# Weight sums of a seven-product feed-forward made by accumulating transfers, two pairs interleaved at its start

## The chip, the cores and the metric

The kernel runs on one core of one Trainium2 chip. The metric is device time in microseconds (us) of one execution; the time before is the median of three runs. The core has a matrix engine (TensorE, "PE" in the profile, with "PEld" for its weight loads), a vector engine (VectorE, "DVE"), an activation engine (ScalarE, "ACT"), a general engine (GpSimd, "POOL") and SyncE ("SP"), which here only issues transfers. Each engine takes its own instructions in program order and waits on semaphores for the others. PSUM is the memory that PE writes; it has eight banks.

## The reference

One inference step of a two-layer streaming encoder on 576 token columns (512 of a prompt, 64 of a sample), model width 1024. Each layer has a half-step feed-forward, a mixer (attention with a gated convolution in layer 0, a state-space mixer in layer 1), cross attention over 256 memory tokens, and a second half-step feed-forward:

```python
def swiglu(x, w_gu, w_down):
    gate, up = jnp.split(x @ w_gu, 2, axis=-1)
    return (jax.nn.silu(gate) * up) @ w_down

x = x + 0.5 * swiglu(rms_norm(x, ln_ffn1[l]), w_ffn1_gu[l], w_ffn1_down[l])
...
x = x + 0.5 * swiglu(rms_norm(x, ln_ffn2[l]), w_ffn2_gu[l], w_ffn2_down[l])
```

The hidden width is 2816, that is 22 tiles of 128. All arrays are float32.

## The kernel before

**Numbers as two parts.** PE is fed with pairs of numbers: `hi` (L136) lets ACT write a rounded copy, `lo` (L142) lets DVE write the rest. A product is then three matmuls per tile of 128 rows: high by high, high by low, low by high.

**Tokens in columns.** X is held transposed: eight tiles (f = 0 to 7) of 128 model rows by 576 columns. The columns are worked on in two halves of 288.

**Three of the four feed-forwards use seven products instead of eight.** For ffn2 of layer 0, ffn1 of layer 1 and ffn2 of layer 1 (`gain`, L496), a *pair* is a gate tile and an up tile of weights, 128 hidden columns each, `g1` and `g2`, each stored as 128 x 1024. Cutting the model rows into halves gives four weight blocks of 128 x 512: A11 and A12 in `g1`, A21 and A22 in `g2`. With two halves of the columns this is a 2 x 2 block product, and the kernel makes it in the Winograd form: seven products with four sums of weight blocks, four sums of x, and sums of the results. Product k uses weight `pr.src[k]`: k = 0 is A11, k = 2 is A12, k = 6 is A22, and k = 1, 3, 4, 5 are sums. `pair_ops` (L327) gives the matching halves of x: k = 0 and 1 use model tiles f < 4, k = 2 and 5 use f >= 4, and k = 3, 4, 6 use the sums `eh`, `el` of both. A product is 12 matmuls (`one`, L313) and writes one of the pair's three banks T, Y, W; `PLACE` lists them: k = 0, 3, 4, 6 go to T one after the other, 1 and 5 to Y, 2 to W. Before k = 3 may add to T, ACT must have copied what k = 0 left there, and so on; `pair_epi` (L534) makes these copies and additions after each product.

**Weight sums.** `pair_load` (L276) has SP load `g1` into a tile `r1` (tag wraw, three buffers that all other weights use too) and `g2` into `r2` (tag raw2, three buffers). `pair_sum` (L285) has DVE make the four sums, 128 x 512 each, into six buffers (tag ss). `run_steps` emits them up to six products ahead of `prep`, the place where ACT and DVE write the high and low parts of a product's weights. Two products share one weight buffer, of which there are three, so the parts are written some four products before PE uses them.

**Order.** `pair_steps` (L296) gives every product a place: pair n's product k stands at 7n + at[k], and all are sorted. A feed-forward is done in three parts of 6, 8 and 8 pairs (`PARTS`); each part is followed by eight down products of 48 (or 36) matmuls. In `run_steps` each product is a step: first the weights of later steps are loaded and prepared (`issue`, `ahead`, `prep`), then PE's matmuls are emitted, then the epilogue. At most three weight loads are open at a time (`st["open"]`).

**The start of a paired feed-forward.** It follows a layer whose last eight tiles of X come in the order 0, 4, 1, 5, 2, 6, 3, 7 (`PAIRED`). As each tile is done on PE, DVE adds it to X (L1315 after cross attention, L656 after a feed-forward), and `finalize_s` (L333) makes its high and low parts, the sums of x, and its squares. The first pair's k = 0 needs f = 0 to 3, its k = 2 needs f = 7 too. The norm's factor R is not known yet at that time: it is made beside the first products (`stats_tok`, ten matmuls of L471; `diag`, L444; `stats_bcast`, ten matmuls of L455), and the first pair's gate is multiplied by R later (`st["first"]`).

Of the kernel before, what the change touches and what calls it, by code (L numbers as in the profile page):

```python
# [9 lines left out]
F32 = mybir.dt.float32  # L10
# [3 lines left out]
ALU = mybir.AluOpType  # L14
# [7 lines left out]
HF = 288  # L22
# [48 lines left out]
class Pair:  # L71


    def __init__(self, g1, g2):
        self.g = (g1, g2)


class Kernel:
# [77 lines left out]
    def run_steps(self):  # L156
# [13 lines left out]
        def issue():  # L170
            i = st["issued"]
            g = items[i]
            if part[i]:
                if g.k == 0:
                    if self.fs is None or st["open"] >= 3 or i > st["prepped"] + 7:
                        return False
                    st["open"] += 1
                    self.pair_load(g.pair)
# [15 lines left out]
        def prep():  # L194
# [13 lines left out]
            if part[i]:  # L208
                c = slice(512 * place[i][1], 512 * place[i][1] + 512)
# [4 lines left out]
                self.lo(l, src, h)  # L214
            else:
# [7 lines left out]
        def ahead(n):  # L223
            while st["issued"] < min(st["prepped"] + n, N) and issue():
                pass
            while st["summed"] < min(st["issued"], st["prepped"] + 6):
                i = st["summed"]
                if part[i]:
                    self.pair_sum(items[i].pair, items[i].k)
                st["summed"] += 1  # L230

        used = 0
        for fn, gs, limit in self.steps:
# [6 lines left out]
            elif used < N:  # L240
                top = place[used][0] + (2 if gs else 1)
                while st["prepped"] < N and place[st["prepped"]][0] <= top:
# [3 lines left out]
                    ahead(8 if part[i] else 3)  # L246
                    prep()
                if here or (st["prepped"] < N and part[min(st["prepped"] + 2, N - 1)]):
                    ahead(8)
# [14 lines left out]
    def fs_open(self):  # L264
        if self.fs is None:
# [4 lines left out]
            fs["sum"] = self.phase_pool(fs, "fss", 6)  # L270
# [5 lines left out]
    def pair_load(self, pr):  # L276
        r1 = self.wraw.tile([128, WG], F32, tag="wraw", name="wraw")
        r2 = self.fs["raw"].tile([128, WG], F32, tag="raw2", name="raw2")
        self.nc.sync.dma_start(r1, pr.g[0])
        self.nc.sync.dma_start(r2, pr.g[1])  # L280
        a11, a12, a21, a22 = r1[:, :512], r1[:, 512:], r2[:, :512], r2[:, 512:]
        pr.src = [a11, None, a12, None, None, None, a22]
        pr.a21 = a21

    def pair_sum(self, pr, k):  # L285
        if k not in (1, 3, 4, 5) or pr.src[k] is not None:
            return
        for d in {3: (1,), 5: (3,)}.get(k, ()):
            self.pair_sum(pr, d)
        a11, s1, a12, s2, s3, s4, a22 = pr.src  # L290
        x, y, op = {1: (pr.a21, a22, ALU.add), 3: (s1, a11, ALU.subtract), 4: (a11, pr.a21, ALU.subtract),
                    5: (a12, s2, ALU.subtract)}[k]
        t = pr.src[k] = self.fs["sum"].tile([128, 512], F32, tag="ss", name="ss")
        self.nc.vector.tensor_tensor(t, x, y, op=op)  # L294

    def pair_steps(self, grans, ops, epi, late):  # L296
# [5 lines left out]
        for n, (g1, g2) in enumerate(grans):  # L302
# [30 lines left out]
    def finalize_s(self, f, gain):  # L333
# [14 lines left out]
        if f < 4:  # L348
            d = self.tmp("tb", HF)
            V.tensor_tensor(d, X[:, f, two], X[:, f, one], op=ALU.subtract)  # L350
# [6 lines left out]
        else:  # L357
# [5 lines left out]
            V.tensor_tensor(t[:, two], t[:, one], x0[:, one], op=ALU.add)  # L363
            self.hi(h, X[:, f], scale=g)
            V.scalar_tensor_tensor(u, X[:, f, one], g, t[:, two], op0=ALU.mult, op1=ALU.subtract)
            self.hi(e, t2)
            self.hi(self.eh[:, 2, k], u)
            self.lo(l, X[:, f], h, scale=g)
            self.lo(self.el[:, 0:2, k], t2, e)
            self.lo(self.el[:, 2, k], u, self.eh[:, 2, k])  # L370
# [158 lines left out]
    def ffn(self, gu, dn, gain_next, pairs=True, early=False):  # L529
# [4 lines left out]
        def pair_epi(k, pr, first, last, scaled):  # L534
# [5 lines left out]
            if k == 0:  # L540
# [4 lines left out]
                if "first" in st:  # L545
                    st["dg"] = self.diag(st["r"], "td")
            elif k == 1:
                self.hi(pr.tb[:, two], Y)
                if "first" in st:
                    st["R"] = self.stats_bcast(None, dg=st.pop("dg"), ps=self.banks[:, 6:8])  # L550
                    st.pop("first")()
            elif k == 3:
                self.hi(pr.tc[:, one], T)
                if first:
                    tt(pr.ta[:, two], Y, pr.tc[:, one], op=ALU.add)
# [1837 lines left out]
```

## Time and profile before

| | before |
|---|---|
| median of 3 runs | 2525.88 us (2524.17 to 2526.79) |
| the profiled execution | 2526.99 us, its span 2525.2 us |
| mean granted TensorE clock | 0.991 |
| DVE busy | 1741.2 us |
| POOL busy | 349.3 us |
| HBM read | 245.07 MB |

In a busy row of the page an engine's time is followed by its share of the span and its number of instructions. Matmuls overlap in the pipeline, so the duration of one in a timeline is longer than the time from one to the next. In the chain of waits a row is start, duration, engine, the tile written and the line; "x672" counts merged instructions. In a timeline the bracket at the end of a row gives how long the engine stood idle before it and what released it. In a table of windows each engine's busy time is followed by its number of instructions; the last three columns are granted clock, busy share of the DMA engines, and GB/s.

### The profile page before, as it was taken

The page shows a single profiled execution, that of the slowest core. Times are in us where ns is not written, and L with a number is a line of the kernel's source. Part 1 is how long each engine was busy: PE and PEld are TensorE (multiplying, and loading weights), DVE is VectorE, ACT ScalarE, POOL GpSimd, SP SyncE. Part 2 cuts the span into 40 slices and gives each one's busy share as a digit, 9 for nine tenths or more (in the row PEclk, how much of TensorE's full clock was granted, in tenths as well). Part 3 has the DMA queues.
Part 4 walks back from the last instruction along what each step waited for, and adds up shares of the span by engine and source line. Part 5 has one row for each costly group of instructions (what it writes and reads, how often), then busy time and mean ns, then how long its engine had stood idle before and what let it go on. Part 6 is the DMA issues. An engine that isn't in the chain of part 4 may idle for free.

```text
span 2525.2 us, 44952 instructions
## 1 busy us (share of the span) xinstructions
PE 2472.1 (98%) x18499; PEld 2435.2 (96%) x18499; DVE 1741.2 (69%) x2960; ACT 1074.6 (43%) x1847; POOL 349.3 (14%) x469
## 2 busy tenths in 40 slices
PE   8999999999999999999999999999999999999998
PEld 8998999999899999999999999999999999999998
DVE  5644658667875578786978785965743467787694
ACT  5322222334654455453545352542353355444353
POOL 1576235302420000000000000012310000000001
PEclk9999999999999999999999999999999999999999
DMA  4465653321134322322232323245872222232221
GB/s 149 93 187 184 155 123 122 121 93 36 37 113 136 120 84 70 115 79 97 76 101 61 108 83 101 85 143 167 289 244 84 84 93 84 76 110 84 100 84 64
DMA packets 112557, 279.95 MB, mean 111 GB/s; under 512 B 16304, under 2 KB 45152, under 8 KB 111712
## 3 DMA queue, kind: packets, MB, share of 16 engines
q1 hardware_dynamic: 112352, 277.08, 35.0%
q8 instruction: 145, 2.38, 0.4%
q14 instruction: 60, 0.49, 0.1%
HBM read 245.07 MB, written 31.97 MB: 110 GB/s over the span
## 4 chain that ended last, share of the span: by engine, by line
PE 75%; DVE 11%; DMA 5%; ACT 4%; POOL 2%; issue 2%; SPq 1%; ACTq 0%; POOLq 0%; DVEq 0%
PE banks L398 35%; PE banks L319 28%; PE banks L667 2%; PE banks L1912 2%; DVE wl L219 2%; DMA b<-in_ssm_bw 1%; PE banks L1293 1%; PE banks L1261 1%; PE banks L2188 1%; PE banks L1808 1%; ACT wh L138 1%; DVE ss L294 1%; POOL w L1414 1%; PE banks L1595 1%; DVE mx L999 1%
## 5 line engine op out<-in xcount | busy, mean ns | idle before, releaser
L138 ACT ACTIVATE wh<-wraw 128x1024 fp32r<-128x1024 f32 (+3 forms) x411 | 352.3, 861 | 331.9 <-PE banks L398 177.5
L219 DVE TENSOR_TENSOR wl<-wraw,wh 128x1024 fp32r<-128x1024 f32 (+2 forms) x264 | 321.6, 1221 | 171.9 <-ACT wh L138 169.7
L398 PE MATMUL banks<-hh,wh 128*128 128x288 f32 x1768 | 379.6, 296 | 2.6 <-ACT hh L138 1.8
L398 PE MATMUL banks<-hh,wl 128*128 128x288 f32 x1768 | 378.8, 296 | 2.8 <-DVE wl L219 2.8
L398 PE MATMUL banks<-hl,wh 128*128 128x288 f32 x1768 | 378.7, 296 | 0.5 <-DVE hl L144 0.5
L319 PE MATMUL banks<-xh,wh 128*128 128x288 f32 x1056 | 313.7, 297 | 7.9 <-ACT tb L138 4.0
L319 PE MATMUL banks<-xl,wh 128*128 128x288 f32 x1056 | 313.5, 297 | 3.6 <-DVE xl L146 3.4
L319 PE MATMUL banks<-xh,wl 128*128 128x288 f32 x1056 | 313.3, 297 | 0.4 <-DVE wl L144 0.4
L398 PEld LDWEIGHTS banks<-hh,wh 128*128 128x128 f32 x1768 | 284.7, 189 | 4.2 <-ACT hh L138 2.3
L398 PEld LDWEIGHTS banks<-hh,wl 128*128 128x128 f32 x1768 | 284.8, 189 | 3.2 <-DVE wl L219 3.2
L398 PEld LDWEIGHTS banks<-hl,wh 128*128 128x128 f32 x1768 | 284.8, 189 | 1.0 <-DVE hl L144 1.0
L398 PE MATMUL banks<-xh,wh 128*128 128x288 f32 x1232 | 269.3, 300 | 10.2 <-ACT wh L138 9.3
L398 PE MATMUL banks<-xh,wl 128*128 128x288 f32 x1232 | 267.4, 299 | 4.0 <-DVE wl L219 3.9
L398 PE MATMUL banks<-xl,wh 128*128 128x288 f32 x1232 | 266.1, 298 | 0.0
L319 PE MATMUL banks<-eh,wh 128*128 128x288 f32 x792 | 235.3, 297 | 1.0 <-DVE tc L579 1.0
L319 PE MATMUL banks<-el,wh 128*128 128x288 f32 x792 | 234.8, 296 | 0.0
L319 PE MATMUL banks<-eh,wl 128*128 128x288 f32 x792 | 234.5, 296 | 0.0
L144 DVE TENSOR_TENSOR wl<-ss,wh 128x512 fp32r<-128x512 f32 x264 | 181.4, 689 | 49.7 <-ACT wh L138 47.9
L398 PEld LDWEIGHTS banks<-xh,wh 128*128 128x128 f32 x1232 | 200.9, 191 | 12.2 <-ACT wh L138 9.6
L319 PEld LDWEIGHTS banks<-xh,wh 128*128 128x128 f32 x1056 | 200.0, 189 | 9.4 <-ACT tb L138 4.8
L398 PEld LDWEIGHTS banks<-xh,wl 128*128 128x128 f32 x1232 | 200.9, 191 | 5.7 <-DVE wl L219 5.5
L319 PEld LDWEIGHTS banks<-xl,wh 128*128 128x128 f32 x1056 | 199.9, 189 | 4.7 <-DVE xl L146 4.7
(539 smaller groups left out, 4927.0 us busy)
## 6 DMA issues: line engine op xcount, KB each, us to landing
wraw<-in_gu SPq DMA_DIRECT2D x110, 512.0 KB
raw<-in_gu SPq DMA_DIRECT2D x66, 512.0 KB
wraw<-in_dn SPq DMA_DIRECT2D x64, 512.0 KB
wraw<-in_dn SPq DMA_DIRECT2D x32, 384.0 KB
wraw<-in_win SPq DMA_DIRECT2D x17, 512.0 KB
wraw<-in_xq SPq DMA_DIRECT2D x16, 512.0 KB
wraw<-in_xk SPq DMA_DIRECT2D x16, 512.0 KB
wraw<-in_xv SPq DMA_DIRECT2D x16, 512.0 KB
```

Source lines behind the costliest of these rows:

```text
L138: self.nc.scalar.activation(out, in_, AF.Copy)
L144: self.nc.vector.tensor_tensor(out, in_, hi.bitcast(F32), op=ALU.subtract)
L219: self.lo_engine.tensor_tensor(l[:p, :n], t[:p, :n], h[:p, :n].bitcast(F32), op=ALU.subtract)
L294: self.nc.vector.tensor_tensor(t, x, y, op=op)
L319: mm(out, ww[:, ws], xx[:, kk], start=k < 3 and kk == 0 and pi == 0, stop=kk == 3 and pi == 2, skip_group_check=True)
L398: mm(ps[:M, h, :n], ww[:, k * M:(k + 1) * M], xx[:, k0 + k, h * n:(h + 1) * n], start=first and k == 0 and pi == 0, stop=last and k == kt ...
L667: nc.tensor.matmul(ps, ww[:, k * 128:(k + 1) * 128], xx[:, k, c0:c0 + n], start=k == 0 and pi == 0, stop=k == KT - 1 and pi == 2)
L999: V.reduce_max(mx[:m, qt:qt + 1], out, axis=AX.X)
L1261: mm(out, x[:, k, t * 128:t * 128 + m], y[:, k], start=k == 0 and pi == 0, stop=k == 1 and pi == 2)
L1293: mm(out, x[:, k, f * 128:(f + 1) * 128], y[:, k, ts], start=k == 0 and pi == 0, stop=k == 1 and pi == 2)
L1414: e.tensor_tensor(o_i, ar, bi, op=ALU.mult)
L1912: mm(ps[:, h, :HF], ww[:, k * 128:(k + 1) * 128], xx[:, k, h * HF:(h + 1) * HF], start=k == 0 and pi == 0, stop=k == 7 and pi == 2)
```

## The change

It concerns the three paired feed-forwards only.

- **Weight sums.** The signs of the Winograd form are turned, so that three of the four sums become plain additions. `pair_ahead` has POOL issue a transfer that adds A22, read from HBM, onto A21 in `r2` (for k = 1). After k = 1's parts are written, `pair_sums` has DVE make one sum (for k = 3, now two buffers), and POOL issue a transfer that adds A21, read from HBM, onto A11 in `r1` (for k = 4). After k = 2's parts, POOL issues one that adds the sum of k = 3, from SBUF, onto A12 in `r1` (for k = 5). Each is 128 x 512 float32, 256 KB. The signs are put right in `finalize_s` and in the down products' factor, -0.5.
- **Order.** The usual order of a pair becomes 0, 1, 2, 3, 5, 4, with its k = 6 between the next pair's 3 and 5. The first two pairs of a feed-forward are interleaved: first pair (a), second pair (b): a0 a1 b0 b1 a2 b2 a3 a5 b3 a4 b5 b4 a6 b6.
- **Look-ahead.** Loads may be issued when k = 0 stands up to 11 products ahead instead of 7; the sums' emission is five products ahead instead of six.
- **Norm factor.** Statistics still follow the first pair's k = 3; diag moves from the second pair's k = 0 to the first's k = 5, the broadcast and the first gate from the second's k = 1 to its k = 3.

```diff
-                    if self.fs is None or st["open"] >= 3 or i > st["prepped"] + 7:
+                    if self.fs is None or st["open"] >= 3 or i > st["prepped"] + 11:
...
                 self.hi(h, src)
                 self.lo(l, src, h)
+                self.pair_sums(g.pair, g.k)
...
-            while st["summed"] < min(st["issued"], st["prepped"] + 6):
+            while st["summed"] < min(st["issued"], st["prepped"] + 5):
                 i = st["summed"]
                 if part[i]:
-                    self.pair_sum(items[i].pair, items[i].k)
+                    self.pair_ahead(items[i].pair, items[i].k)
...
-                    ahead(8 if part[i] else 3)
+                    ahead(12 if part[i] else 3)
...
-            fs["sum"] = self.phase_pool(fs, "fss", 6)
+            fs["sum"] = self.phase_pool(fs, "fss", 2)
...
+        pr.src = [pr.r1[:, one], pr.r2[:, one], pr.r1[:, two], None, pr.r1[:, one], pr.r1[:, two], pr.r2[:, two]]
+
+    def pair_ahead(self, pr, k):
+
+        if k == 1:
+            self.nc.gpsimd.dma_start(pr.r2[:, pr.half[0]], pr.g[1][:, pr.half[1]], accum_op=ALU.add)
+
+    def pair_sums(self, pr, k):
+
+        one, two = pr.half
+        if k == 1:
+            t = pr.src[3] = self.fs["sum"].tile([128, 512], F32, tag="ss", name="ss")[:, one]
+            self.nc.vector.tensor_tensor(t, pr.r2[:, one], pr.r1[:, one], op=ALU.add)
+            self.nc.gpsimd.dma_start(pr.r1[:, one], pr.g[1][:, one], accum_op=ALU.add)
+        elif k == 2:
+            self.nc.gpsimd.dma_start(pr.r1[:, two], pr.src[3], accum_op=ALU.add)
...
-            at = {0: 0, 1: 1, 3: 3, 2: 4, 5: 5, 4: 6, 6: 9}
-            if n == len(grans) - 1:
-                at = {0: 0, 1: 1, 3: 3, 2: 4, 4: 5, 5: 6, 6: 7}
-            elif late and n == 0:
-                at = {0: 0, 1: 1, 2: 2, 5: 3, 3: 4, 4: 7.5, 6: 10.5}
+            at = {0: 0, 1: 1, 2: 2, 3: 3, 5: 5, 4: 6, 6: 11}
+            if late and n < 2:
+                at = ({0: 0, 1: 1, 2: 4, 3: 6, 5: 7, 4: 9, 6: 12}, {0: -5, 1: -4, 2: -2, 3: 1, 5: 3, 4: 4, 6: 6})[n]
+            elif n == len(grans) - 1:
+                at = {0: 0, 1: 1, 2: 2, 3: 3, 5: 5, 4: 6, 6: 9}
...
-            V.tensor_tensor(d, X[:, f, two], X[:, f, one], op=ALU.subtract)
+            V.tensor_tensor(d, X[:, f, one], X[:, f, two], op=ALU.subtract)
...
-            V.tensor_tensor(t[:, two], t[:, one], x0[:, one], op=ALU.add)
+            V.scalar_tensor_tensor(t[:, two], t[:, one], -1.0, x0[:, one], op0=ALU.mult, op1=ALU.subtract)
...
+            elif k == 3:
+                self.hi(pr.tc[:, one], T)
+                if first:
+                    st["r"] = self.stats_tok(self.acc, self.ones, 1.0, ps=self.banks[:, 6:8])
+                elif "first" in st:
+                    st["R"] = self.stats_bcast(None, dg=st.pop("dg"), ps=self.banks[:, 6:8])
+                    st.pop("first")()
...
+                tt(pr.ta[:, two], Y, pr.tc[:, one], op=ALU.add)
                 if first:
                     st["first"] = lambda: (gate(), self.defer(silu, 1))
-                    return
-                tt(pr.ta[:, two], Y, pr.tc[:, one], op=ALU.add)
-                if last:
+                    st["dg"] = self.diag(st["r"], "td")
+                elif last:
```

More of the change, by code (lines that the diff above doesn't have):

```diff
@@ L75, in __init__ @@
         self.g = (g1, g2)
+        self.kw = g1.shape[1] // 2
+        self.half = slice(0, self.kw), slice(self.kw, 2 * self.kw)
 class Kernel:
@@ L208, in prep @@
             if part[i]:
-                c = slice(512 * place[i][1], 512 * place[i][1] + 512)
+                c = slice(512 * place[i][1], 512 * place[i][1] + g.pair.kw)
                 src = g.pair.src[g.k]
@@ L245, in run_steps @@
                         break
-                    ahead(8 if part[i] else 3)
+                    ahead(12 if part[i] else 3)
                     prep()
                 if here or (st["prepped"] < N and part[min(st["prepped"] + 2, N - 1)]):
-                    ahead(8)
+                    ahead(12)
             ws = [handles.pop(used + k) for k in range(len(gs))]
@@ L276, in pair_load @@
     def pair_load(self, pr):
[L277 to L286, printed above, removed]
-            return
[L288 to L294, printed above, removed]
+        n = 2 * pr.kw
+        pr.r1 = self.wraw.tile([128, WG], F32, tag="wraw", name="wraw")
+        pr.r2 = self.fs["raw"].tile([128, WG], F32, tag="raw2", name="raw2")
+        self.nc.sync.dma_start(pr.r1[:, :n], pr.g[0])
+        self.nc.sync.dma_start(pr.r2[:, :n], pr.g[1])
+        one, two = pr.half
[4 more added lines that the diff above has]
+    def pair_sums(self, pr, k):
+        one, two = pr.half
+        if k == 1:
[4 more added lines that the diff above has]
+            self.nc.gpsimd.dma_start(pr.r1[:, two], pr.src[3], accum_op=ALU.add)
     def pair_steps(self, grans, ops, epi, late):
@@ L362, in finalize_s @@
             V.scalar_tensor_tensor(t[:, one], X[:, f, two], g, x0[:, two], op0=ALU.mult, op1=ALU.subtract)
-            V.tensor_tensor(t[:, two], t[:, one], x0[:, one], op=ALU.add)
+            V.scalar_tensor_tensor(t[:, two], t[:, one], -1.0, x0[:, one], op0=ALU.mult, op1=ALU.subtract)
             self.hi(h, X[:, f], scale=g)
-            V.scalar_tensor_tensor(u, X[:, f, one], g, t[:, two], op0=ALU.mult, op1=ALU.subtract)
+            V.scalar_tensor_tensor(u, X[:, f, one], g, t[:, two], op0=ALU.mult, op1=ALU.add)
             self.hi(e, t2)
-            self.hi(self.eh[:, 2, k], u)
+            self.hi(self.eh[:, 2, k], u, scale=-1.0)
             self.lo(l, X[:, f], h, scale=g)
             self.lo(self.el[:, 0:2, k], t2, e)
-            self.lo(self.el[:, 2, k], u, self.eh[:, 2, k])
+            self.lo(self.el[:, 2, k], u, self.eh[:, 2, k], scale=-1.0)
         if f == 0:
@@ L544, in pair_epi @@
                 self.hi(pr.tb[:, one], T)
-                if "first" in st:
-                    st["dg"] = self.diag(st["r"], "td")
             elif k == 1:
                 self.hi(pr.tb[:, two], Y)
[L549 to L554, printed above, removed]
-                    tt(pr.ta[:, two], Y, pr.tc[:, one], op=ALU.add)
-                    st["r"] = self.stats_tok(self.acc, self.ones, 1.0, ps=self.banks[:, 6:8])
             elif k == 2:
@@ L655, in down @@
                 if last and pairs:
-                    V.scalar_tensor_tensor(self.h2(x), ps[:, :, :HF], 0.5, self.h2(x), op0=ALU.mult, op1=ALU.add)
+                    V.scalar_tensor_tensor(self.h2(x), ps[:, :, :HF], -0.5, self.h2(x), op0=ALU.mult, op1=ALU.add)
                 else:
                     t = self.tmp("tc")
-                    V.scalar_tensor_tensor(self.h2(t), ps[:, :, :HF], 0.5, self.h2(st["R"]), op0=ALU.mult, op1=ALU.mult)
+                    V.scalar_tensor_tensor(self.h2(t), ps[:, :, :HF], -0.5 if pairs else 0.5, self.h2(st["R"]), op0=ALU.mult, op1=ALU.mult)
                     V.tensor_tensor(x, x, t, op=ALU.add)
@@ L671, in down_out @@
                 x = self.X[:, f, c0:c0 + n]
-                V.scalar_tensor_tensor(x, ps, 0.5, x, op0=ALU.mult, op1=ALU.add)
+                V.scalar_tensor_tensor(x, ps, -0.5, x, op0=ALU.mult, op1=ALU.add)
                 if f == 0 and c0 == 0:
```

2 lines of the change are left out of this document (removed).

## The prediction

> **What bounds the kernel now.** I read the page's engine shares first, then the chain that ended last in order of time, then the timelines of DVE, ACT and PE around the starts of the three paired feed-forwards.
>
> ```profile
> PE 2472.1 (98%) x18499; PEld 2435.2 (96%) x18499; DVE 1741.2 (69%) x2960; ACT 1074.6 (43%) x1847; POOL 349.3 (14%) x469
> ```
>
> PE leaves 53 us of the span idle, so nothing here can gain more than a few per cent. The chain says where it can. A piece that is PE for tens of microseconds has no gap in it:
>
> ```profile
> 935.73 0.99 PE banks L471 x10
> 936.72 4.97 PE banks L319 x36
> 941.68 1.25 PE banks L455 x10
> ...
> 954.60 43.15 PE banks L319 x324
> 997.75 38.40 PE banks L398 x288
> 1036.14 89.02 PE banks L319 x672
> 1125.16 51.19 PE banks L398 x384
> ...
> 1393.14 38.40 PE banks L398 x288
> ...
> 2191.75 38.40 PE banks L398 x288
> ```
>
> 672 matmuls in 89.02 us are 56 products of 12, so a product takes 1.59 us and a pair of seven 11.13. From 954.60 to the end of that feed-forward PE never waits, so fewer DVE sums can gain nothing there. What is left is its first part, six pairs, 42 products: 42 x 1.5896 = 66.76 us, plus the ten small matmuls of L471 (0.99) and of L455 (1.25) that each feed-forward has once: 69.0 us without a wait. The first product starts here (PE timeline):
>
> ```profile
> 919.84 0.19 PEld L319 LDWEIGHTS banks<-xh,wh 128*128 128x128 f32 x1
> 1316.26 0.19 PEld L319 LDWEIGHTS banks<-xh,wh 128*128 128x128 f32 x1
> 2113.37 0.19 PEld L319 LDWEIGHTS banks<-xh,wh 128*128 128x128 f32 x1
> ```
>
> The part ends where the down products begin: 997.75 - 919.84 = 77.9, 1393.14 - 1316.26 = 76.9, 2191.75 - 2113.37 = 78.4 us. Against 69.0 that is 8.9, 7.9 and 9.4: **26.2 us lost at three starts**, all that this change can win from PE. Two kinds of loss, seen in the first:
>
> ```profile
> 926.84 0.19 PEld L319 LDWEIGHTS banks<-xh,wh 128*128 128x128 f32 x1 [1.72 <-ACT xh L140]
> 928.37 0.29 PEld L319 LDWEIGHTS banks<-xl,wh 128*128 128x128 f32 x1 [1.33 <-DVE xl L146]
> 930.34 0.29 PEld L319 LDWEIGHTS banks<-xh,wh 128*128 128x128 f32 x1 [1.47 <-ACT tb L138]
> ```
> ```profile
> 929.00:939.00 10.00, 8.88 (x53) 8.63 (x53) 8.26 (x21) 5.79 (x13) 0.00 (x0) 0.72 0.01 2
> ```
>
> PE waits for the last tile of x (f = 7) and for the copy of T, and the granted clock falls to 0.72 for the ten microseconds after. Behind that stands a late DVE:
>
> ```profile
> 893.29 1.23 DVE L219 TENSOR_TENSOR wl<-wraw,wh 128x1024 fp32r<-128x1024 f32 x1 [0.20 <-ACT wh L138]
> 899.45 0.69 DVE L294 TENSOR_TENSOR ss<-raw 128x512 f32<-128x512 f32 x1 [4.93 <-DMA raw<-in_gu]
> ...
> 901.51 0.75 DVE L1315 TENSOR_TENSOR X<-banks,X 128x576 f32<-128x576 f32 x1
> ...
> 907.35 0.76 DVE L1315 TENSOR_TENSOR X<-banks,X 128x576 f32<-128x576 f32 x1
> ...
> 912.54 0.75 DVE L1315 TENSOR_TENSOR X<-banks,X 128x576 f32<-128x576 f32 x1
> ...
> 917.25 0.69 DVE L144 TENSOR_TENSOR wl<-wraw,wh 128x512 fp32r<-128x512 f32 x1
> ...
> 919.66 0.75 DVE L1315 TENSOR_TENSOR X<-banks,X 128x576 f32<-128x576 f32 x1
> ...
> 923.43 0.68 DVE L144 TENSOR_TENSOR wl<-wraw,wh 128x512 fp32r<-128x512 f32 x1
> 924.03 0.69 DVE L294 TENSOR_TENSOR ss<-ss,wraw 128x512 f32<-128x512 f32 x1
> 925.23 0.75 DVE L1315 TENSOR_TENSOR X<-banks,X 128x576 f32<-128x576 f32 x1
> ...
> 929.94 0.69 DVE L144 TENSOR_TENSOR wl<-ss,wh 128x512 fp32r<-128x512 f32 x1
> ```
>
> The out products take 48 matmuls, 6.4 us (51.19 / 8), a tile. Counted back from 919.84, PE is done with f = 5, 2, 6, 3, 7 at 894.2, 900.6, 907.0, 913.4, 919.8; DVE adds them to X at 901.51, 907.35, 912.54, 919.66, 925.23, some 5.4 to 7.3 late. It stood 4.93 us in front of a pair sum that waited for its weights, and made six sums, the first at 899.45, the last at 924.03.
>
> **The change, part by part.** *Sums off DVE.* Three feed-forwards have 22 pairs each. 3 x 66 sums of 0.69 (the row at 899.45) = 137 us leave DVE. In the gapless stretches they hide under PE and are worth nothing. At a start they count: the sum that stood 4.93 us now comes behind its own pair's second product, and 2 sums instead of 6 stand before f = 7. New DVE timetable from the distances of the rows above (such instructions follow each other every 0.60, 923.43 to 924.03): f = 5 from 894.2, 5.84 of work (901.51 to 907.35): 900.0. f = 2 from 900.6, 5.19: 905.8. f = 6 from 907.0, 4.71: 911.7, then the first pair's two low parts and its one sum, 1.8: 913.5. f = 3, 3.77 (919.66 to 923.43): 917.3, the second pair's three: 919.1. f = 7 is then added as PE delivers it, 919.8 instead of 925.23.
>
> *Products in another order.* Before, two products (k = 0, 1) need only the tiles f < 4; the third needs f = 7. Now the two pairs give four: 4 x 1.59 = 6.4 us of work from 919.8 to 926.2. xh and xl of f = 7 come 1.6 and 3.1 us behind its add (926.84 and 928.37 against 925.23), at 921.4 and 922.9. So neither stops PE. k = 3 adds onto T; five products lie between it and the first pair's k = 0 where three did, so the copy of T is done too. Without an idle PE I take the clock to stay at the 1.00 it has elsewhere.
>
> *What is moved.* The broadcast of R (L455) comes two products after the statistics (3.18 us), where 4.97 lay between. diag is late by:
>
> ```profile
> 939.24 1.03 DVE L444 TENSOR_SCALAR dg<-ident,tko 128x128 f32<-128x128 f32 x5
> ```
>
> It ends 3.55 us after L471 does (936.72), so some 0.4 us of waiting. gate and silu of the first pair move with it; its k = 6 ends four products after the broadcast, 6.4 us for a multiplication and an activation. The next user of the first pair's banks now comes one product (1.59 us) after its k = 6, not three and a half; it waits for one DVE product, and with the sums gone DVE has no queue there. The sign changes put one instruction of DVE for another of its size. Loads may be issued eleven products ahead instead of seven, but three buffers limit them as before. The last pair of each part has k = 6 behind k = 4 instead of k = 5, which gives its silu one product more. Together I leave **1.5 us a start** on PE.
>
> *Three accumulating transfers a pair, 256 KB each, issued by POOL.* POOL does nothing in these stretches, so its queue is free; a pair's two late transfers stand there ahead of the next pair's early one, which waits only for a load that landed long before. No row shows such a transfer. Call L the time from the last reader's end to its landing. Bounds:
>
> ```profile
> L1584 POOL TENSOR_TENSOR ca<-x,sr 128x1152 f32<-128x1152 f32 x8 | 21.6, 2704 | 68.3 <-DMA s5wout<-ca 55.5 <-DVE wl L219 12.8
> ```
> ```profile
> b<-in_ssm_bw SPq DMA_DIRECT2D x8, 512.0 KB
> ...
> s5y<-yw SPq DMA_DIRECT2D x3, 592.0 KB
> ...
> yr<-s5y SPq DMA_DIRECT2D x24, 74.0 KB
> ```
> ```profile
> 178.31 3.50 DMA b<-in_ssm_bw
> ...
> 1827.74 2.24 DMA yr<-s5y
> ...
> 1837.65 9.66 DMA s5y<-yw
> ```
>
> Low: nothing for POOL and a 74 KB transfer, 2.24 us. High: its longest instruction 2.7 + the slow 592 KB store 9.66 = 12.4 us. An accumulate reads its 256 KB and the target's 256 KB, so the 512 KB load at 3.50 is nearest; with 1.0 for POOL I take **L = 4.5 us**. The Trainium skill, DMA: Bandwidth & Descriptors, section on the anatomy of one DMA, fits about 2.0 us plus size over 436 GB/s for a transfer issued by GpSimd, an estimate of 2.6 us; no run here shows it, and by it the sum stays as it is.
>
> Who waits for L? The transfer into the second half of the first weight row (for k = 5) is sent behind k = 2 and used three products later; that is the short one. k = 4's has five, and k = 1's is sent ahead. hi of k = 5 waits at the head of ACT, and the copies out of the banks and the next hi stand behind it. In steady state the weights run ahead:
>
> ```profile
> 1069.55 0.41 ACT L138 ACTIVATE tb<-banks 128x288 f32<-128x288 f32 x1 [0.15 <-PE banks L319]
> ```
> ```profile
> 1069.71 0.69 DVE L144 TENSOR_TENSOR wl<-wraw,wh 128x512 fp32r<-128x512 f32 x1
> ```
>
> k = 0 ended just before the copy at 1069.55; k = 2 then started about 4.77 later, 1074.3, and its low part was ready at 1070.4: 3.9 ahead.
> ```profile
> L138 ACT ACTIVATE wh<-ss x264: 613/622/638, 916.4 to 2450.2; 128x512 fp32r<-128x512 f32 x132
> ```
>
> So L may be 3.9 + 3 x 1.59 - 1.3 (hi and lo of k = 5, 0.62 and 0.69) = 7.4 us before PE waits, once a pair. At a start the low part of k = 2 follows the 4.71 of f = 7 (925.23 to 929.94): done at 919.8 + 4.7 + 0.7 = 925.2; PE wants k = 5 at 919.8 + 7 x 1.59 + 0.99 = 931.9, so L may be 5.4. At 4.5 both hold and the transfers cost nothing; their cover is that lead.
>
> **Sum.** 26.2 - 0.4 (a load starts 0.14 before its matmul) - 3 x 1.5 = 21 us won. The profiled execution took 2526.99 (span 2525.2 and 1.8 around it), 1.1 above the median of the runs, 2525.88; from the median: **2505 us**.
>
> **Rivals.** *The wait comes back in part*: L between 5.4 and 7.4. Each start loses up to 2.0 us at the first pair's k = 5, as much at the second's, and the clock may fall again, about 4 x 3 = 12 us: **2517**. For it: the start has the least lead, and two pairs' megabytes are loading then. Against: the loads are issued long before.
>
> *The transfers become the bound, slower*: L above 7.4 us at k = 5. It decides from 7.4 + 21/66 = 7.7 us on; at L = 9 each of 66 pairs loses 1.6, 106 us, against a gain that shrinks to some 10: **2620**; at the high bound, 66 x 5.0, above 2840. For it: one high row, 9.66, a third queue of requests on DMA engines that also carry 1 MB of weights a pair. Against: those are busy a quarter of the time here, with POOL at zero:
>
> ```profile
> 1060.00:1110.00 50.00, 50.00 (x379) 50.00 (x379) 44.71 (x81) 29.08 (x56) 0.00 (x0) 1.00 0.27 85
> ```
>
> *POOL is held off while DVE computes*: DVE is busy 44.71 of 50, after the change 44.7 x (1 - 3 x 0.6 / 9.95) = 36.6, in runs of up to 8 us. A transfer that had to wait out such a run adds about 4 us: L = 8.5, 66 x 1.1 = 73, **2585**. No row speaks for or against it, since POOL does nothing in these stretches; its one high price would be that of the case before. The Trainium skill, SBUF — State Buffer, on who interferes with whom, has GpSimd's descriptor writing blocked by DVE's two-port modes but, by inference, not by tensor_tensor; nearly all of DVE's work here is that, so by the page this rival falls away. No run here shows it.
>
> *DVE was not the cause*: the starts stay late because PE delivers f = 7 last and four products do not cover what follows: **2525**, no change. Against: the timetable above.
>
> **Chances.** Forecast, gain over 15 us: 0.52. Part of it: 0.20. No change: 0.08. Transfers the bound: 0.13. POOL held off: 0.07. About 0.2% (5 us) is what a measurement of this kernel tells from no change. Faster 0.71, same 0.09, slower 0.20. The range holds the first three: from 26.2 us won with nothing left, **2499**, to 5 above the median, **2531**; the slower cases lie outside.
>
> **What would show it.** Right: no idle PE between the first product of a feed-forward and its down products, 69 to 71 us instead of 77 to 78; clock 1.00 there; X for f = 7 added within 1 us of PE's end; DVE near 1605 us busy; waits of ACT for the accumulates short. Wrong: ACT's hi of k = 5 or DVE behind it waiting for the transfer in every pair, with PE gaps at 11-us intervals; POOL's issues spread over microseconds; PE waiting for L444 or for the bank copies at the starts.

## The result and the profile after

The changed kernel takes **2562.44 us**, median of 4 runs (2562.05 to 2565.37), beside 2526.09 (2524.17 to 2526.79) for the kernel before: ratio 1.0148, 95% interval 1.0130 to 1.0165. It is 36 us slower; 2505 with a range of 2499 to 2531 was predicted. The profiled execution took 2562.18, span 2560.1, mean granted clock 0.989.

Page of the kernel after: engine shares and the issues of POOL's transfers, whose last number is the median from issue to landing.

```profile
PE 2477.1 (97%) x18499; PEld 2438.1 (95%) x18499; DVE 1628.7 (64%) x2762; ACT 1066.3 (42%) x1847; POOL 524.1 (20%) x667
...
raw<-in_gu POOLq DMA_DIRECT2D x66, 256.0 KB, 5.5
wraw<-in_gu POOLq DMA_DIRECT2D x66, 256.0 KB, 4.1
wraw<-ss POOLq DMA_DIRECT2D x66, 256.0 KB, 4.5
```

DVE has lost 112 us of work and the transfers land about as estimated, yet the span grew. PE has the same 18499 instructions, so it stands still somewhere new. Waits of PE in the kernel after (total, times, longest), then one of ACT:

```profile
PE banks L327 <- DVE tc L584: 35.5, 12, 4.3
...
PE banks L327 <- ACT tb L141: 2.5, 4, 1.0
...
ACT wh L141 <- DMA wraw<-ss: 140.3, 61, 6.4
```

The first row is the loss. L584 is DVE's addition of what k = 4 left in bank T to the copy that ACT made before. Nine of its twelve waits are 3.4 to 4.3 us long, 34.1 together, one at the end of each of the nine parts (three feed-forwards of three parts); the other three are 0.5 us each, at the starts. ACT waits 140 us for the transfer of k = 5, and in the middle of a part of eight pairs PE takes no harm from it. Windows of the kernel after: PE busy, PEld, DVE, ACT, POOL, granted clock, DMA share, GB/s.

```profile
1060.00:1110.00 50.00, 50.00 (x379) 50.00 (x378) 36.86 (x67) 28.24 (x55) 10.56 (x12) 1.00 0.71 157
```

PE is gapless there as before, DVE went from 44.71 to 36.86 (36.6 was predicted), the share of the DMA engines from 0.27 to 0.71.

The end of a part in the kernel after, here the second part of the first paired feed-forward: PE, then DVE, then ACT.

```profile
1124.61 0.29 PE L327 MATMUL banks<-eh,wl 128*128 128x288 f32 x1
1128.29 0.41 PE L327 MATMUL banks<-eh,wh 128*128 128x288 f32 x1 [3.39 <-DVE tc L584]
```
```profile
1123.91 0.46 DVE L568 TENSOR_TENSOR ta<-ta,R 128x288 f32<-128x288 f32 x1
1126.64 1.23 DVE L223 TENSOR_TENSOR wl<-wraw,wh 128x1024 fp32r<-128x1024 f32 x1 [2.27 <-ACT wh L141]
1127.78 0.45 DVE L584 TENSOR_TENSOR tc<-banks,tb 128x288 f32<-128x288 f32 x1
```
```profile
1124.40 0.68 ACT L571 ACTIVATE ta<-ta 128x576 f32<-128x576 f32 x1 [2.89 <-DVE ta L568]
1124.99 0.67 ACT L141 ACTIVATE hh<-td 128x576 fp32r<-128x576 f32 x1
1125.57 1.04 ACT L141 ACTIVATE wh<-wraw 128x1024 fp32r<-128x1024 f32 x1
```

The last matmul of k = 4 starts at 1124.61. k = 6 goes to the same bank T, directly behind it, and has to wait until L584 has read the bank. L584 itself is free to run at 1124.9, but DVE works in program order, and in front of it stands the low part of a down product's weights (L223), which waits 2.27 us for its high part on ACT. ACT in turn made the silu that follows k = 5 first (L571, released by DVE at 1124.4), then the high part of a hidden tile (hh), then the weights' 1.04 us. So the bank is read at 1127.78 instead of some three microseconds earlier. In the kernel before, k = 5, which goes to bank Y, stood between the two, and the same read came in time (kernel before, PE's last matmul of k = 4 and first of k = 6, then DVE):

```profile
1121.66 0.30 PE L319 MATMUL banks<-eh,wl 128*128 128x288 f32 x1
...
1123.39 0.32 PE L319 MATMUL banks<-eh,wh 128*128 128x288 f32 x1
```
```profile
1120.79 1.23 DVE L219 TENSOR_TENSOR wl<-wraw,wh 128x1024 fp32r<-128x1024 f32 x1 [2.13 <-ACT wh L138]
...
1122.80 0.45 DVE L579 TENSOR_TENSOR tc<-banks,tb 128x288 f32<-128x288 f32 x1
```

The wide low part waits 2.13 us there too, but that wait is over before k = 4 is done: no silu stands in front of its high part on ACT, because the silu belongs to k = 5 and comes later (L566 at 1125.94). The read ends at 1123.25, 1.29 us behind k = 4 and 0.14 before k = 6 starts. So the swap did two things: it took away the 1.59 us of k = 5 that covered the read, and it made the read later, 3.3 to 4.3 us behind k = 4 at the nine ends of the kernel after, 0.8 to 1.3 in the kernel before.

PE's time from the first product of a part to the last, from the starts in its timeline (the floor is 69.0 for a first part with its 20 small matmuls, 89.0 for one of eight pairs):

| | first parts | parts of eight pairs |
|---|---|---|
| before | 77.6, 76.6, 78.1 | 89.0, six times |
| after | 77.3, 78.7, 77.1 | 92.7, 94.7, 94.0, 94.7, 94.0, 94.7 |

The six long parts lose 30.8 us, the first parts 0.8: they win at the start nearly what they lose at the end. The spans of the two profiled executions, 2525.2 and 2560.1, differ by 34.9 us. Of the 3.3 that are left, nearly 3 lie in the down products behind the parts, the rest in other stages.

### The profile page after: what moved, and what is told of

Its sections match the earlier page's. It is cut to its first block, busy times and chain, and to the rows that moved or that the text cites. A ratio compares the mean times of both kernels' runs of the same rounds, so it can differ in the third digit from the quotient of the medians.

```text
span 2560.1 us, 45526 instructions
## 1 busy us (share of the span) xinstructions
PE 2477.1 (97%) x18499; PEld 2438.1 (95%) x18499; DVE 1628.7 (64%) x2762; ACT 1066.3 (42%) x1847; POOL 524.1 (20%) x667
## 5 line engine op out<-in xcount | busy, mean ns | idle before, releaser
L141 ACT ACTIVATE wh<-wraw 128x512 fp32r<-128x512 f32 (+2 forms) x543 | 430.3, 803 | 506.5 <-PE banks L406 229.7
L223 DVE TENSOR_TENSOR wl<-wraw,wh 128x1024 fp32r<-128x1024 f32 (+2 forms) x264 | 322.4, 1224 | 168.6 <-ACT wh L141 166.4
L327 PE MATMUL banks<-xh,wh 128*128 128x288 f32 x1056 | 312.0, 295 | 1.3 <-ACT tb L141 0.8
L327 PE MATMUL banks<-xh,wl 128*128 128x288 f32 x1056 | 311.4, 295 | 0.0
L327 PE MATMUL banks<-xl,wh 128*128 128x288 f32 x1056 | 310.9, 294 | 0.0
L327 PE MATMUL banks<-eh,wh 128*128 128x288 f32 x792 | 238.8, 302 | 37.2 <-DVE tc L584 35.5
L147 DVE TENSOR_TENSOR wl<-wraw,wh 128x512 fp32r<-128x512 f32 x264 | 181.4, 688 | 144.9 <-ACT wh L141 131.7
L327 PE MATMUL banks<-el,wh 128*128 128x288 f32 x792 | 237.6, 300 | 0.0
L327 PE MATMUL banks<-eh,wl 128*128 128x288 f32 x792 | 237.3, 300 | 0.0
L327 PEld LDWEIGHTS banks<-xh,wh 128*128 128x128 f32 x1056 | 198.4, 188 | 2.6 <-DVE td L605 1.4
```

Of the source, the lines that this page charges most:

```text
L141: self.nc.scalar.activation(out, in_, AF.Copy)
L147: self.nc.vector.tensor_tensor(out, in_, hi.bitcast(F32), op=ALU.subtract)
L223: self.lo_engine.tensor_tensor(l[:p, :n], t[:p, :n], h[:p, :n].bitcast(F32), op=ALU.subtract)
L327: mm(out, ww[:, ws], xx[:, kk], start=k < 3 and kk == 0 and pi == 0, stop=kk == 3 and pi == 2, skip_group_check=True)
```

## The experiments

Theory A: the loss is the order at the end of each part (k = 4 and k = 6 back to back in bank T). Theory B, the rival: the accumulating transfers are the bound, that is the waits of ACT for them and the third stream of requests.

| label | start | sums | end of part | median us | ratio to before, 95% |
|---|---|---|---|---|---|
| after | interleaved | transfers | 5, 4, 6 | 2562.4 | 1.0148 [1.0130, 1.0165] |
| e1_k4_first | interleaved | transfers | 4, 5, 6 | 2524.6 | 0.9995 [0.9985, 1.0005] |
| e2_before_k5_first | as before | DVE | 5, 4, 6 | 2570.6 | 1.0189 [1.0174, 1.0205] |
| e3_dve_sums | interleaved | DVE | 4, 5, 6 | 2539.7 | 1.0063 [1.0050, 1.0075] |
| e4_usual_start | usual | transfers | 4, 5, 6 | 2508.0 | 0.9935 [0.9922, 0.9947] |
| e8_dve_usual | usual | DVE | 4, 5, 6 | 2524.6 | 0.9995 [0.9986, 1.0005] |
| e12_usual_start_alone | usual | transfers | 5, 4, 6 | 2550.9 | 1.0099 [1.0076, 1.0122] |
| e7_k6_earlier | usual | transfers | 4, 5, 6, pair before sooner | 2521.8 | 0.9989 [0.9979, 1.0000] |
| e11_rest_sooner | usual | transfers | 4, 5, 6, a low part sooner | 2501.6 | 0.9901 [0.9886, 0.9915] |
| e9_pool_one | usual | transfers, 1 copy ahead | 4, 5, 6 | 2509.5 | 0.9939 [0.9922, 0.9955] |
| e10_pool_three | usual | transfers, 3 copies ahead | 4, 5, 6 | 2634.6 | 1.0419 [1.0404, 1.0434] |

### The order at the end of a part

**e1_k4_first**, the kernel after with the last pair's k = 4 put ahead of its k = 5, nothing else:

```diff
             elif n == len(grans) - 1:
-                at = {0: 0, 1: 1, 2: 2, 3: 3, 5: 5, 4: 6, 6: 9}
+                at = {0: 0, 1: 1, 2: 2, 3: 3, 4: 5, 5: 6, 6: 9}
```

> The changed kernel, but in the last pair of each of the nine parts k = 4 stands before k = 5, as it did before the change. Theory A (the order at the end of a part): the changed kernel's PE waits 35.5 us in all before k = 6 for the addition of L584 that reads T, 3.5 to 4.5 us at each of the nine part ends, and some 8 to 11 us more go to the low clock after it; with a product between k = 4 and k = 6 both go, 2562 - 46 = 2516, and every part of eight pairs takes 89.0 us again. Theory B (the accumulating transfers are the bound: ACT waits 140 us for them): nothing of that goes, 2555 to 2565.

Measured: 2524.59 us (2519.53 to 2528.97, 11 runs), 37.9 below the kernel after (46 were expected), and not to be told from the kernel before. The parts of eight pairs take 89.0 to 89.7 again. Waits of PE:

```profile
PE banks L327 <- ACT tb L141: 3.1, 4, 2.0
...
PE banks L463 <- DVE dg L452: 3.0, 4, 1.1
...
PE banks L327 <- DVE td L605: 1.9, 3, 1.2
PE banks L327 <- DVE tc L584: 1.8, 4, 0.5
```

35.5 us of waiting for L584 became 1.8. All transfers are still there, so B can't explain the 36 us.

**e2_before_k5_first**, the other way round: the kernel before, with the last pair's k = 5 put ahead of its k = 4. The kernel before has no accumulating transfer at all.

```diff
             if n == len(grans) - 1:
-                at = {0: 0, 1: 1, 3: 3, 2: 4, 4: 5, 5: 6, 6: 7}
+                at = {0: 0, 1: 1, 3: 3, 2: 4, 5: 5, 4: 6, 6: 7}
```

> The kernel before with one line changed: in the last pair of each part k = 5 stands before k = 4, so that k = 6 follows k = 4 at once. All sums stay on DVE, no transfer is added. Theory A: k = 6 waits for T at nine part ends, 3.5 to 5 us each, and the clock falls after it: 2526 + 35 to 50 = 2561 to 2576. Theory B: no transfers, no loss, 2526.

Measured: 2570.56 us (4 runs), ratio 1.0189. The one swap makes the kernel before slower by 44 to 45 us, and the wait of PE has the same name:

```profile
PE banks L319 <- DVE tc L579: 29.8, 12, 3.5
```

The parts of eight pairs take 92.8 to 94.0, the first parts 3.0 to 3.6 more than before. Theory A is shown from both sides.

### What the transfers and the interleaving are worth

With k = 4 first, e1 still gains nothing over the kernel before. **e3_dve_sums** takes e1 and makes all four sums on DVE again (six buffers, emitted ahead, as before the change; the new signs and orders stay):

```diff
-                self.pair_sums(g.pair, g.k)
...
-                    self.pair_ahead(items[i].pair, items[i].k)
+                    self.pair_sum(items[i].pair, items[i].k)
...
+        x, y = {1: (pr.r2[:, one], pr.r2[:, two]), 3: (pr.src[1], pr.r1[:, one]), 4: (pr.r1[:, one], pr.r2[:, one]),
+                5: (pr.r1[:, two], pr.src[3])}[k]
+        t = pr.src[k] = self.fs["sum"].tile([128, 512], F32, tag="ss", name="ss")
+        self.nc.vector.tensor_tensor(t, x, y, op=ALU.add)
```

> As the first run (k = 4 first at the end of a part, two pairs interleaved at the start), but all four sums are made by DVE in buffers of their own, as before the change; no accumulating transfer. Tells what the transfers bring by themselves. Theory A: the order does most of what the starts gain, the sums on DVE make it late again in part; parts of eight pairs stay at 89.0 us, starts lose between the 4.2 us of the changed kernel and the 8.4 of before: 2517 to 2529. Theory B: without transfers it is faster than the first run by tens of us.

**e4_usual_start** takes e1 and drops the interleaving: only the first pair's k = 6 is held back, to the second pair's k = 5.

```diff
-            if late and n < 2:
-                at = ({0: 0, 1: 1, 2: 4, 3: 6, 5: 7, 4: 9, 6: 12}, {0: -5, 1: -4, 2: -2, 3: 1, 5: 3, 4: 4, 6: 6})[n]
+            if late and n == 0:
+                at = {0: 0, 1: 1, 2: 2, 3: 3, 5: 5, 4: 6, 6: 12.5}
```

> As the first run, with the accumulating transfers, but the first two pairs of a feed-forward are not interleaved: the first pair has the usual order 0, 1, 2, 3, 5, 4 and its k = 6 late, the second the usual order. Theory A with my prediction's reading of the starts: the third product needs the last tile of x again, some 3 us a start more than the first run (xl of the last tile comes 3.1 us after PE delivers it, and two products of 1.59 stand before instead of four), with the clock falling after it perhaps 5: 2525 to 2531. If instead the late DVE alone made the starts slow, and the sums' move cured it, it is the first run's time within 3 us.

**e8_dve_usual** is e4 with e3's sums on DVE, the fourth corner.

```diff
-                self.pair_sums(g.pair, g.k)
...
-                    self.pair_ahead(items[i].pair, items[i].k)
+                    self.pair_sum(items[i].pair, items[i].k)
```

> The fourth corner: usual start, k = 4 first at the end of a part, and all four sums on DVE as before the change, no accumulating transfer. With interleaved pairs the transfers were worth 2539.7 - 2524.6 = 15 us. If they are worth the same here, 2508 + 15 = 2523, the time of the kernel before. If the order of products alone made the gain, 2508; if the sums on DVE hurt only beside interleaved pairs, 2508 to 2514.

Measured: e3 2539.68 (5 runs), e4 **2507.99** (2505.2 to 2509.77, 5 runs), e8 2524.64 (10 runs). e3 lies above the 2517 to 2529 expected for it, and e4 16.6 below e1, where the expectation had at best e1's time. So the transfers are worth 2539.7 - 2524.6 = 15.1 us with the interleaving and 2524.6 - 2508.0 = 16.7 without it; the interleaving *costs* 16.6 with transfers and 15.0 without. The two add up, and in the kernel after the gain of the one paid for the other. e8 still has the new usual order, the signs, the longer look-ahead and the moved norm factor, and can't be told from the kernel before (0.9995): together these are worth nothing that shows.

e4's start has next to no gap. Its chain of waits around the first part:

```profile
920.47 6.34 PE banks L327 x48
...
927.81 8.15 PE banks L327 x60
...
935.97 0.40 ACT tb L141
...
939.52 51.07 PE banks L327 x384
990.59 38.40 PE banks L406 x288
```

990.59 - 920.47 = 70.1 us against 77.6 before (all three: 70.1, 70.3, 69.6). 48 matmuls, four products, go through without a gap though only two of them can do without f = 7. DVE's timeline in e4 says why:

```profile
920.51 0.76 DVE L1320 TENSOR_TENSOR X<-banks,X 128x576 f32<-128x576 f32 x1 [1.23 <-PE banks L406]
...
922.78 0.81 DVE L149 SCALAR_TENSOR_TENSOR xl<-X,vecs,xh 128x576 fp32r<-128x576 f32 x1
```

The low part of f = 7 is done at 923.59. The third product starts at about 920.3 + 2 x 1.59 = 923.5, and comes to f = 7 only in its last quarter, at 924.7. The two products of cover were enough once DVE was in time.

In e1 the first parts take 73.2, 75.6 and 72.5: 11.3 us of the 16.6 that the interleaving costs. The other five lie in stages that neither edit touches (before the first start, and between the second and the third feed-forward). Single executions differ there without the interleaving too: the first paired product starts at 920.3 in e4, 923.6 in e1 and 925.5 in e9, which has e4's start. So the five aren't shown to be the interleaving's. In its first parts e1's PE waits 8.9 us in all, e4's 1.1. Of the 8.9, the norm's diag makes 2.5. The second pair's k = 6 waits 0.5 at each start for the read of what its k = 4 left in T, two products before. The fifth pair's k = 0 waits 1.9 in all for the read of the third pair's k = 6 in the same bank. The last 3.1 are copies of banks of the third and fourth pair (tb), which stand on ACT behind a high part of k = 5 that waits for its transfer. Here it is at the third pair (ACT, kernel after; e1 starts a feed-forward in the same order):

```profile
951.03 0.63 ACT L141 ACTIVATE wh<-wraw 128x512 fp32r<-128x512 f32 x1 [4.04 <-DMA wraw<-ss]
```

The third pair's k = 5 follows its k = 3 at once, since the k = 6 that the usual order puts between them went ahead with the interleaved pairs. No run takes these waits apart; some 3.5 of the 11.3 us are in no wait of this list.

**e12_usual_start_alone** makes e4's edit of the start in the kernel after and leaves the end of a part as it is there.

```diff
-            if late and n < 2:
-                at = ({0: 0, 1: 1, 2: 4, 3: 6, 5: 7, 4: 9, 6: 12}, {0: -5, 1: -4, 2: -2, 3: 1, 5: 3, 4: 4, 6: 6})[n]
+            if late and n == 0:
+                at = {0: 0, 1: 1, 2: 2, 3: 3, 5: 5, 4: 6, 6: 12.5}
```

> The changed kernel with one thing undone: the first two pairs of a feed-forward are not interleaved; at the end of a part k = 5 still stands before k = 4. If the two losses are separate, the starts win the 11 to 17 us that the interleaving cost in the comparison of the other two runs, and the part ends still lose their 46: 2562 - 11 to 17 = 2545 to 2551.

Measured: 2550.93 (4 runs), 11.5 below the kernel after. The parts of eight pairs lose as in the kernel after (92.7 to 95.5), the first parts win 3.5 to 5.1 each: the two losses lie in different places. So three pairs of runs price the interleaving, at 16.6, 15.0 and 11.5 us.

### How near the transfers are to being the bound

**e9_pool_one** and **e10_pool_three** delay the transfer for k = 5: POOL copies the low part of k = 2's weights to a buffer that nothing reads, once or three times, ahead of that transfer. They add work and leave none out.

```diff
         elif k == 2:
+            for _ in range(3):
+                self.nc.gpsimd.tensor_copy(self.fs["sum"].tile([128, 512], F32, tag="idle", name="idle"), l.bitcast(F32))
             self.nc.gpsimd.dma_start(pr.r1[:, two], pr.src[3], accum_op=ALU.add)
```

(In e9 the range is 1.)

> The run with the usual start; before POOL issues the transfer for k = 5 it makes one copy of the low part of k = 2 that nothing reads, 128x512, some 1.4 us (the page of before has 0.78 for 128x256 on POOL). That makes L, the time from the low part of k = 2 to the landing, some 1.4 us longer, 6 to 7 us. By my prediction's bound of 7.4 us in the steady order and 5.4 at a start, the parts of eight pairs stay at 89.0 us and the starts lose up to 1.5 us each: 2508 to 2513. If the transfers stand at their limit already, every pair loses some 1.4: 2508 + 66 x 1.4 = 2600.

> The same with three copies, some 4.2 us: L becomes 8.6 to 9.6, beyond 7.4. By the bound each of 66 pairs loses 1.2 to 2.2 us: 2508 + 80 to 145 = 2590 to 2655, with PE waiting for ACT's or DVE's part of k = 5. If the weights run further ahead than I worked out, 2508 to 2520.

Measured: e9 2509.53 (4 runs), 1.5 above e4 and inside e4's spread; e10 2634.63 (4 runs), 126.6 above e4, 1.9 us for each of 66 pairs. From the end of k = 2's low part (the last reader) to the start of the high part that waits for the landing, medians over the pairs where ACT waited: e4 5.0 us, e9 5.1, e10 7.9. One copy took POOL 0.6 us where 1.4 was expected, and made the landing only 0.1 later, so e9 hardly tests anything. Waits of PE in e10, and one of ACT:

```profile
PE banks L329 <- ACT tb L141: 54.3, 36, 3.5
...
ACT wh L141 <- DMA wraw<-ss: 272.8, 64, 6.8
```

ACT stands for its transfers twice as long as in the kernel after. PE doesn't wait for the weights of k = 5 but for the bank copies that stand behind them on ACT. So B's mechanism exists, and it decides somewhere between 5.1 and 7.9 us; in the parts of eight pairs the transfers as the change issues them stay below that point.

### What is left at the end of a part

e4 shows one new wait of 3.0 us at the end of the last feed-forward (PE at its output product, for the low part of the last pair but one):

```profile
PE banks L672 <- DVE hl L147: 3.0, 1, 3.0
```

**e7_k6_earlier** puts that pair's k = 6 two products sooner, ahead of the last pair's k = 2:

```diff
+            elif n == len(grans) - 2:
+                at = {**at, 6: 9}
```

> The run with the usual start and k = 4 first at the end of a part, and k = 6 of the last pair but one stands two products earlier again (between the last pair's k = 1 and 2, as before the change). In the run it starts from, PE waits 3.0 us at the first down product of the last feed-forward for a low part of the hidden tiles on DVE, and 1.9 us in all at the other parts. If that wait is the deferred low part of the last pair but one, it goes: 2508 - 3 to 5 = 2504. If it is the last pair's own low part, nothing changes: 2508.

Measured: 2521.82 (12 runs), 13.8 *above* e4. With that k = 6 gone from its place, the last pair's k = 4 follows directly on k = 3, and both go to T:

```profile
PE banks L329 <- ACT tc L141: 13.9, 9, 3.8
```

It is the same fault with another pair of products: nine waits, one at the end of each part, for the copy of T (tc) that ACT makes after k = 3. In all nine it stands behind the high part of a down product's weights, and that behind a hidden tile's high part (hh), which waits for DVE. The last of the nine (ACT, e7):

```profile
2447.28 0.68 ACT L141 ACTIVATE hh<-td 128x576 fp32r<-128x576 f32 x1 [1.76 <-DVE td L610]
2447.88 1.04 ACT L141 ACTIVATE wh<-wraw 128x1024 fp32r<-128x1024 f32 x1
2448.82 0.39 ACT L141 ACTIVATE tc<-banks 128x288 f32<-128x288 f32 x1
```

DVE in turn was late because it stood at the low part of k = 5, whose high part had waited 1.97 us for its transfer.

**e11_rest_sooner** leaves the order alone and only emits the low part of the last pair but one a step sooner:

```diff
+            pr.late = n == len(grans) - 2
...
-                    self.defer(rest, 1)
+                    self.defer(rest, 0 if pr.late else 1)
```

> The run with the usual start and k = 4 first (2508), and the deferred low part of the hidden tile of the last pair but one is emitted one step sooner. If the 3.0 us that PE waits at the first down product of the last feed-forward, and the 1.9 us at the other parts, are for that low part, behind the last pair's own work on DVE, they go: 2503 to 2505. If they are the last pair's own low part: 2508, no change.

Measured: **2501.63 us** (2500.36 to 2504.76, 4 runs), beside 2526.65 for the kernel before, ratio 0.9901 [0.9886, 0.9915]: 25 us faster than before and 61 faster than after. The wait at the output product is gone; through the last two parts of the third feed-forward and to the output products the chain is PE without a gap:

```profile
2207.44 89.05 PE banks L328 x672
2296.49 51.19 PE banks L407 x384
2347.68 89.14 PE banks L328 x672
2436.82 10.56 PE banks L673 x72
```

## Why the prediction was wrong

**The step that failed** is in "what is moved": "The last pair of each part has k = 6 behind k = 4 instead of k = 5, which gives its silu one product more", left inside 1.5 us a start. I asked what k = 6 gains from its distance to k = 5 and not what it loses against k = 4. Both write T; before, a product for another bank (1.59 us) stood between them and covered the read of T. That read also got later, since the silu of k = 5 now goes first on ACT. The stall is 3.4 to 4.3 us in nine places, 34.1 us, where 1.5 at each of three starts was left. In all but one of the six long parts, matmuls at half the rate follow (clock, below), and there the part is 5.0 to 5.7 us longer. e1 and e2 show it by taking out and putting in this one swap. The rows of the kernel before, shown above, gave the warning, with the read of T done 0.14 us before k = 6; by them alone, with the read 0.8 to 1.3 us behind k = 4, the nine ends would have come to some 10 us, an estimate. The rest comes from the queue on ACT, which has to be followed in the new order. The prediction names what is queued behind a wait for k = 5's weights, and asks no such thing at the end of a part, where the trace of before showed no gap.

**Where the 26.2 us lie: right.** e4's three first parts take 210.0 together, 232.3 before: 22.3 won; e11's 209.5, or 22.8, against the 21 of the sum. On the whole e11 gains 25.0 and e4 17.8; e4 gives 3.0 back at the output product, and stages that the change doesn't touch differ by microseconds from run to run.

**The cause of the loss, a late DVE: right.** The kernel after, DVE:

```profile
894.87 0.76 DVE L1320 TENSOR_TENSOR X<-banks,X 128x576 f32<-128x576 f32 x1
...
914.19 0.75 DVE L1320 TENSOR_TENSOR X<-banks,X 128x576 f32<-128x576 f32 x1
...
920.47 0.76 DVE L1320 TENSOR_TENSOR X<-banks,X 128x576 f32<-128x576 f32 x1 [0.63 <-PE banks L406]
...
922.74 0.81 DVE L149 SCALAR_TENSOR_TENSOR xl<-X,vecs,xh 128x576 fp32r<-128x576 f32 x1
```

The five adds come within 0.8 us of PE's ends as predicted (894.2, 900.6, 907.0, 913.4, 919.8), the last 4.8 sooner than before, and xl of f = 7 is done 3.1 behind its add. But I gave the credit to "DVE in time" and "four products of cover" together. e4 shows that the first alone does it: the other two products of cover were not needed, and the interleaving that provides them costs 11 to 17 us. The prediction's own numbers said so: xl ready at 922.9, while with two products of cover PE comes to f = 7 in the last quarter of the third, at 919.8 + 2.75 x 1.59 = 924.2.

**The residue of 1.5 us a start: mis-sized.** e1, whose parts end without the fault, has first parts 4.2, 6.6 and 3.5 above the floor. The waits that I named are among them: for the reads of banks, of which I wrote that DVE has no queue there (L605 and L584 together 3.7 us, and 3.1 for ACT's L141), and for diag, 3.0 in four where 0.4 a start was estimated.

**L = 4.5 us: half a microsecond short.** From the last reader's end it is 5.0 in the median: 0.4 until POOL issues (1.0 was assumed) and 4.5 from issue to landing (3.3 to 6.3; 3.5 was assumed). The other two transfers take 4.1 and 5.5 from issue to landing. The Trainium skill, DMA: Bandwidth & Descriptors, section on the anatomy of one DMA, gives by its fit 2.6 us, an estimate; the accumulating transfers here take 1.5 to 2.9 more.

**The lead of 7.4 us: too wide.** e10 loses 1.9 us a pair at 7.9 us. If a microsecond more costs a microsecond, the transfers decide from about 6.0 on, an estimate; since the copies of e10 also slowed DVE (below) it may be up to half a microsecond higher. The end of the lead is not the use of k = 5's weights, as I reckoned it, but the bank copies behind it on ACT.

**The rivals.** None came true. The transfers were not the bound (e1, e4), though the margin was nearer 1 us than the 2.9 between 4.5 and 7.4. POOL was not held off by DVE (last section). The wait was in part back at the starts, by way of the third and fourth pair's k = 5 and not the first's: 2.5 us of PE in all in the kernel after (L327 for tb), where the rival had 12. The slower case that did come was in no rival.

**Sums off DVE.** DVE 1628.7 instead of near 1605: 198 sums took away 112 us, 0.57 each, where I counted the row's 0.69; by the prediction's rows such instructions follow each other every 0.60, so they overlap, and busy time counts the overlap once.

## What to carry to other kernels

When an order is changed, list for each memory bank who writes it, who has to read it before the next write, and what stands in front of that reader on its own engine; a distance of one product between two writers can be all that hides an in-order queue, and the new order can lengthen that queue too. Price the parts of a change one by one, and ask whether one of them already removes the need for another: here the sums by transfer made the interleaving superfluous, and with it and the swapped end a gain of 18 us showed as a loss of 36. A sum may be moved to an accumulating transfer if the time from the last reader's end to the landing, 5 us here, stays below the lead of everything that is queued behind its first reader.

## What the runs showed of the hardware

**The length of a stall does not settle whether PE goes to half rate after it.** Windows from the end of four waits: two in the kernel after (3.39 us, ending at 1128.29, and 3.44, at 2342.63), then two in e2 (3.52 us each, at 1129.51 and 1684.59). The granted clock is the last number but two:

```profile
1128.00:1131.00 3.00, 2.71 (x20) 2.71 (x21) 1.05 (x3) 0.32 (x1) 0.00 (x0) 1.00 0.60 175
2342.50:2345.50 3.00, 2.87 (x12) 2.87 (x13) 0.07 (x1) 0.00 (x0) 0.00 (x0) 0.50 0.54 175
```
```profile
1129.50:1132.50 3.00, 2.99 (x13) 3.00 (x14) 0.00 (x0) 0.00 (x0) 0.00 (x0) 0.55 0.58 175
1684.50:1687.50 3.00, 2.91 (x22) 2.91 (x23) 1.01 (x4) 0.02 (x1) 0.00 (x0) 1.00 0.72 195
```

Where the clock is 1.00 matmuls follow every 0.13 us, where it is halved every 0.24. Two waits of one length in one program ended differently, and in the kernel before waits of 1.1 to 1.5 us close together were enough (the 0.72 of the prediction's window). What does separate them is where the wait lies. In each trace the slow stretches begin on one grid of 3.413 us: in the kernel after at 996.92, 1273.40, 1403.11 and 1536.23, which are 81, 38 and 39 steps apart. Laid on this grid, the wait of 3.39 us falls into two windows with 1.73 and 1.66 us; the one of 3.44 puts 2.58 us into one. In the paired feed-forwards of all twelve traces, every window at full clock in which PE stood idle for 54% or more was followed by half rate, and none with 51% or less was. In other stages some slow stretches began after less idle time, so the limit is this stage's. The part whose wait kept the clock is 3.7 us longer than its floor, that of 3.44 us 5.0. The Trainium skill, TensorE: Matmul & The Clock Gate, Part 1, gives an idle window of about 3.4 us before the array falls to half rate; the step of the grid agrees with it, but a window idle for a good half was enough here.

**Copies on POOL slow instructions of DVE that have both inputs in SBUF.** Three groups of DVE, in e4 and then in e10, whose copies run beside them (busy, mean ns). The first two have both inputs in SBUF, the third has one in PSUM:

```profile
L568 DVE TENSOR_TENSOR ta<-ta,R 128x576 f32<-128x576 f32 x57 | 43.2, 758 | 3.5 <-ACT R L467 1.6
...
L147 DVE TENSOR_TENSOR wl<-ss,wh 128x512 fp32r<-128x512 f32 x66 | 45.1, 684 | 0.0
...
L584 DVE TENSOR_TENSOR tc<-banks,tb 128x288 f32<-128x288 f32 x66 | 29.7, 450 | 0.9 <-PE banks L327 0.9
```
```profile
L570 DVE TENSOR_TENSOR ta<-ta,R 128x576 f32<-128x576 f32 x57 | 61.7, 1082 | 3.5 <-ACT R L469 1.6
...
L147 DVE TENSOR_TENSOR wl<-ss,wh 128x512 fp32r<-128x512 f32 x66 | 65.6, 994 | 0.0
...
L586 DVE TENSOR_TENSOR tc<-banks,tb 128x288 f32<-128x288 f32 x66 | 29.4, 446 | 0.0
```

758 became 1082 ns and 684 became 994, 38 us on DVE in all (1625.2 to 1663.0); the third group, 50 of whose 66 ran beside a copy, stayed at 450. POOL's issues of transfers did nothing of the kind. Beside a DVE that is busy three quarters of the time an issue as a rule takes 0.86 to 0.88 us where POOL was idle before it, and some 1.17 where it follows another at once (POOL, kernel after):

```profile
1111.91 0.86 POOL L300 DMA_DIRECT2D wraw<-in_gu  x1 [8.27 <-DVE td L605]
1113.02 0.88 POOL L302 DMA_DIRECT2D wraw<-ss  x1 [0.24 <-DVE ta L573]
```

The low part (128x512) and the multiplication (128x576) that DVE makes beside these two issues, at 1111.92 and 1113.01, take 0.69 and 0.76 us as elsewhere. The Trainium skill, SBUF — State Buffer, section on who interferes with whom, says both: an instruction of DVE with two inputs in SBUF contends with GpSimd's reads of SBUF, and tensor_tensor does not hold up descriptor writing. What it only infers of the second, these rows support.
